# State-space stage: the power tables of three quarters, the norm-weight products and a mask product move from VectorE to GpSimd

## The chip, the cores and the metric

The kernel runs on one core of a Trainium2 chip. A core has a matrix engine (TensorE, PE in the profile), a vector engine (VectorE, DVE), a scalar engine (ScalarE, ACT), a general engine (GpSimd, POOL) and a queue engine that mostly issues transfers (SyncE, SP). Each engine takes its own instructions strictly in the order in which they stand in its program, and semaphores order the engines among each other. Data lies in SBUF (128 partitions), matmul results in PSUM. The metric is the device time of one execution in microseconds (us), smaller is better.

## The reference, cut to what matters

Two layers: a state-space (S5) mixer with a gated output projection, then a latent-attention mixer; each is followed by a gated MLP with a width-3 causal convolution. 256 tokens, 2048 channels, float32. The change touches only the first mixer:

```python
dt = exp(log_dt);  ab = exp(dt * a)                  # a complex, per group (128) and state (64)
bb = ((ab - 1) / a) * b                              # input matrix, 16 channels per group
h[t] = ab * h[t-1] + bb @ u[t]                       # u = rmsnorm(x) * g, per group of 16 channels
y[t] = Re(c @ h[t]) + d * u[t]
y = gelu(y);  val, gate = split(y @ w_glu + b_glu);  out = val * sigmoid(gate)
```

## The kernel before, in words

The recurrence is cut into blocks of 8 tokens. For such a block the kernel needs the powers of `ab` from 0 to 8 (times the coefficient of `bb`), called `z` and, copied with signs, `zs`. The 128 groups are handled in 16 rounds of 8 groups; four rounds make a quarter `qt`, and one call of `powers(qt)` makes the table `zs` for the four rounds of a quarter. `powers` is: two memsets on GpSimd, two ScalarE copies into `z`, then three doubling steps of four VectorE products, sums or differences each (12 instructions on 128 x 64 to 128 x 512 floats, each step reading what the last one wrote), and four ScalarE copies from `z` to `zs`.

A round `n` uses these helpers:

- `lead_e(n)` multiplies the table with the fetched matrices `bc[n]` on VectorE into `e1` and `e2` (128 x 1024 each), and a DMA issued by GpSimd adds `e2` onto `e1`. `lead_f(n)` makes `f1` and `f2` in the same way, and every second round the rotations `si`, `co`.
- `part_k(n)` builds the block kernel `K(n)` with TensorE from `f` and `bc`, ScalarE copies it out and writes it to DRAM (`kd`), and SP reads it back in another layout (`TP`).
- `part_e` and `part_v` transpose `e` (`ET`), multiply with the transposed input `U`, and ScalarE copies the result to `vs`. `part_r` and `part_h` rotate, scan and rotate back on VectorE (`R`, `H`). `part_c(n)` needs `TP(n)` and `H(n)`, two rounds after `part_k(n)`.
- After each quarter `part_d` applies the GELU, and matmuls of the output projection (`glu_steps`, weights 1 MB a unit, split by ScalarE into `whi` and by VectorE into `wlo`) fill TensorE between the rounds.

In the text below, K(1), vs(4) or e(9) are these tiles of round 1, 4 or 9; powers(1) is the table of the second quarter.

Ahead of the rounds ScalarE sums the squares of `x` (L135), GpSimd takes the power -1/2 of the mean (`pow` in `rstd`, L117), and `scale_x(rs, qt)` multiplies a quarter of `x` (two tiles X[0] and X[1], both tagged `raw`) by the norm's weights `gX` on VectorE (L358) and by `rs` on ScalarE (L362). The skip weights `dB` are multiplied with a mask (L341).

The order of the instructions on each engine is set when the program is built: a scheduler takes the operations as their inputs are due by its own costs, and `behind(ins)` forces an instruction to stand after another. At run time an engine that waits holds up everything that stands behind.

Of the kernel before, what the change touches and what calls it, by code (L numbers as in the profile page):

```python
# [12 lines left out]
ALU = mybir.AluOpType  # L13
AX = mybir.AxisListType

P = 128
# [28 lines left out]
def tile_trunk(ctx: ExitStack, tc: tile.TileContext, a: dict):  # L45
    nc = tc.nc
    act, dve, pool, pe, sync = nc.scalar, nc.vector, nc.gpsimd, nc.tensor, nc.sync
    cnt = [0]

    def T(pl, shape, dt=F32, tag=None, bufs=None):  # L50
        cnt[0] += 1
        kw = {"bufs": bufs} if bufs else {}
        return pl.tile(shape, dt, tag=tag, name=f"{tag}_{cnt[0]}", **kw)
# [3 lines left out]
    env = {"wp": ctx.enter_context(tc.tile_pool(name="wp", bufs=2)), "wb": 3}  # L57
# [12 lines left out]
    eps_half = cst[:, C_MH : C_MH + 8]  # L70

    def split(hi, lo, src, eng=None):
        act.activation(hi, src, AF.Copy)  # L73
        (eng or dve).tensor_tensor(lo, src, hi.bitcast(F32), op=ALU.subtract)  # L74

    def wunit(src, nk, cols, gain=None, heads=False, slots=(None, None), onpool=()):
        wp, nb = env["wp"], env["wb"]
        raw = T(wp, [P, nk, cols], F32, "raw")
        sync.dma_start(raw, src)
        out = []  # L80
        hk = max(nk // 2, 1)
        for i, h in enumerate(range(0, nk, hk)):
            if slots[i] is None:
                hi = T(wp, [P, hk, cols], F32R, "whi", nb)
                lo = T(wp, [P, hk, cols], F32R, "wlo", nb)
            else:
                pl = env["xp"] if slots[i] < 10 else env["yp"]
                both = T(pl, [P, 2, hk, cols], F32R, f"x{slots[i]}", 1)
                hi, lo = both[:, 0], both[:, 1]
            if heads:  # L90
                v = raw[:, h : h + hk, :].rearrange("p k (h e) -> p k h e", h=2)
                for o, w, e in ((0, 256, slice(0, P)), (256, 128, slice(P, 192))):
                    z = [t[:, :, o : o + w].rearrange("p k (h e) -> p k h e", h=2) for t in (hi, lo)]
                    split(*z, v[:, :, :, e])
            elif gain is None:
                split(hi, lo, raw[:, h : h + hk, :], pool if slots[i] in onpool else None)
            else:
                for k in range(hk):
                    g = gain[:, h + k : h + k + 1]
                    act.activation(hi[:, k, :], raw[:, h + k, :], AF.Copy, scale=g)  # L100
                    dve.scalar_tensor_tensor(
                        lo[:, k, :], raw[:, h + k, :], g, hi[:, k, :].bitcast(F32), op0=ALU.mult, op1=ALU.subtract
                    )
            out.append((hi, lo))
        return hk, out
# [7 lines left out]
    def rstd(tot, width, n):  # L113
        ms = T(sp, [P, width], F32, "rs_ms")
        dve.tensor_scalar(ms, tot, 1.0 / n, EPS, op0=ALU.mult, op1=ALU.add)
        y = T(sp, [P, width], F32, "rs_y")
        pool.tensor_tensor(y, ms, eps_half[:, :width], op=ALU.pow)  # L117
        t = T(sp, [P, width], F32, "rs_t")
        dve.tensor_tensor(t, y, y, op=ALU.mult)
        dve.tensor_tensor(t, t, ms, op=ALU.mult)  # L120
        dve.tensor_scalar(t, t, -0.5, 1.5, op0=ALU.mult, op1=ALU.add)
        r = T(sp, [P, width], F32, "rs_r")
        dve.tensor_tensor(r, t, y, op=ALU.mult)
        return r
# [55 lines left out]
    def behind(ins):  # L180
        return nullcontext() if ins is None else tc.issue_after(ins)
# [89 lines left out]
    def s5(f):  # L271
        with tc.tile_pool(name="s5", bufs=2) as q1, tc.tile_pool(name="dr", bufs=2, space=bass.MemoryType.DRAM) as dr:
# [6 lines left out]
            X = [T(w0, [P, 4, 512], F32, "raw") for _ in range(2)]  # L279
            for k in range(8):  # L280
                sync.dma_start(X[k // 4][:, k % 4, :], a["xs"][k])
            gX = T(q1, [P, 512], F32, "gX", 1)
# [6 lines left out]
            def t1(tag, w=1):  # L289
                return T(q1, [P, w, P], F32, tag, 1)  # L290
# [31 lines left out]
            for k in (1, 2, 4):  # L322
                u = t1("uu", 2)
# [14 lines left out]
            for z in Ds + Hs:  # L338
                pool.memset(z[:, :, 0:1], 0.0)
            dmask = cst[:, C_DM : C_DM + 16]  # L340
            dve.tensor_tensor(  # L341
                dB.rearrange("p (g q) -> p g q", q=16),
                dB.rearrange("p (g q) -> p g q", q=16),
                dmask.unsqueeze(1).to_broadcast([P, 32, 16]),
                op=ALU.mult,
# [9 lines left out]
            def scale_x(rs, qt):  # L355
                c = slice(P * qt, P * qt + P)
                for h in range(2):
                    dve.tensor_tensor(  # L358
                        X[h][:, :, c], X[h][:, :, c], gX[:, c].unsqueeze(1).to_broadcast([P, 4, P]), op=ALU.mult
                    )  # L360
                for s in range(8):
                    act.activation(  # L362
                        Xn[qt][:, :, 16 * s : 16 * s + 16],
                        X[s // 4][:, s % 4, c].rearrange("p (g q) -> p g q", q=16),
                        AF.Copy,
                        scale=rs[:, s : s + 1],
                    )

            def powers(qt):
                ps_ = slice(32 * qt, 32 * qt + 32)  # L370
                z = T(q1, [P, 2, 9, 2, 32], F32, "z", 1)
                pool.memset(z[:, 0, 8, 1, :], 1.0)
                pool.memset(z[:, 1, 8, 1, :], 0.0)
                act.activation(z[:, :, 8, 0, :], cf[:, :, ps_], AF.Copy)
                act.activation(z[:, :, 0, 1, :], L[8][:, :, ps_], AF.Copy)
                for k, o, i, m in ((1, 7, 8, 1), (2, 5, 7, 2), (4, 1, 5, 4)):

                    def v(b):
                        return z[:, :, b : b + m].rearrange("p c m t n -> p c (m t) n")

                    def l(c):
                        return L[k][:, c, ps_].unsqueeze(1).unsqueeze(1).to_broadcast([P, 2, 2 * m, 32])

                    u, w = (T(q1, [P, 2, 8, 32], F32, n, 1)[:, :, : 2 * m, :] for n in ("pu", "pw"))
                    dve.tensor_tensor(u, v(i), l(0), op=ALU.mult)
                    dve.tensor_tensor(w, v(i), l(1), op=ALU.mult)
                    dve.tensor_tensor(v(o)[:, 0], u[:, 0], w[:, 1], op=ALU.subtract)
                    dve.tensor_tensor(v(o)[:, 1], u[:, 1], w[:, 0], op=ALU.add)
                zz = T(q1, [P, 4, 8, 32], F32, "zs")
                act.activation(zz[:, 1], z[:, 1, 0:8, 1, :], AF.Copy, scale=cst[:, C_SG : C_SG + 1])  # L390
                act.activation(zz[:, 2], z[:, 0, 1:9, 0, :], AF.Copy, scale=cst[:, C_NSG : C_NSG + 1])
                act.activation(zz[:, 3], z[:, 1, 1:9, 0, :], AF.Copy, scale=-1.0)
                act.activation(zz[:, 0], z[:, 0, 0:8, 1, :], AF.Copy)
                return zz
# [16 lines left out]
            PB = 32 // NP  # L411
# [26 lines left out]
            def product(tag, bufs, sb, i):  # L438
                h = (sb % PB) * NP
                o = T(q1, [P, NP, 8, 16], F32, tag, bufs)  # L440
                zt = zs[sb // PB][:, i, :, h : h + NP].rearrange("p i n -> p n i").unsqueeze(3).to_broadcast([P, NP, 8, 16])
                dve.tensor_tensor(o, zt, bc[sb][:, i].unsqueeze(2).to_broadcast([P, NP, 8, 16]), op=ALU.mult)  # L442
                return o

            def fetch(n, eng):
                if n < nb:
                    bc[n] = T(q1, [P, 4, NP, 16], F32, "bc", 3)
                    eng.dma_start(bc[n], a["sBC"][n])

            def lead_e(n):  # L450
                if n >= nb:
                    return
                if n % PB == 0:
                    zs[n // PB] = powers(n // PB)
                E[n], e2 = product("e1", 3, n, 0), product("e2", 2, n, 1)
                pool.dma_start(E[n], e2, accum_op=ALU.add)

            def lead_f(n):
                if n >= nb:
                    return  # L460
                F[n] = product("f1", 3, n, 2), product("f2", 3, n, 3)
                if n % FR == 0:
                    si, co = frames(n // FR)
                    for k in range(FR):
                        fr[n + k] = (si[k], co[k])
# [117 lines left out]
            todo, zs, bc, E, F, fr, U, TP, ET, H = [], {}, {}, {}, {}, {}, {}, {}, {}, {}  # L583
            nb = 4 * PB
# [5 lines left out]
            rs = first_norm()  # L590
            for n in range(3):
                fetch(n, sync)
            lead_e(0)
            lead_f(0)
            scale_x(rs, 0)
# [496 lines left out]
    ng = a["norm_g"]  # L1092
    f = f_pair()
    todo = s5(f)
    env["ap"] = ctx.enter_context(tc.tile_pool(name="ap", bufs=1))
    env["xp"] = ctx.enter_context(tc.tile_pool(name="xp", bufs=1))
# [118 lines left out]
```

## Time and profile before

| what | value |
|---|---|
| median of 3 runs | 2155.88 us (2154.35 to 2156.42) |
| the profiled execution | 2150.99 us, span 2149.2 us |
| TensorE busy over the span | 2054.8 us (96%) |
| VectorE busy over the span | 1376.9 us (64%) |
| ScalarE busy over the span | 1093.6 us (51%) |
| GpSimd busy over the span | 32.3 us (2%), 73 instructions |
| granted TensorE clock, mean | 0.990 |

In timeline rows the columns are: start in us from the span's start, duration in us, engine, line, operation, tile written and tiles read, shape, count, and in brackets how long the engine was idle before and who ended that. Rows of groups have the busy sum and the mean in ns behind the bar. Rows of the table by stretch have, for each engine, its busy time and count in that stretch, then TensorE's granted clock and the transfers' share and rate. Lines are those of the kernel before; in the changed kernel the same operations stand two to three lines lower (L385 to L388 become L387 to L390, L485 becomes L487, L509 becomes L511).

### The profile page before, as it was taken

How to read it: one execution, taken by the hardware profiler on the slowest of the kernel's cores; microseconds unless marked ns; L12 is line 12 of the kernel's file. 1: busy time of each engine (PE TensorE's matmuls, PEld its weight loads, DVE VectorE, ACT ScalarE, POOL GpSimd, SP SyncE). 2: the span in 40 equal slices, each digit the busy share in tenths (PEclk: the TensorE clock that was granted, in tenths of full speed). 3: DMA queues.
4: the chain of work that ended last, by engine and by line, in shares of the span. 5: the costliest groups of instructions: out<-in, count | busy, mean ns of one | idle time of the engine just before them, and what ended most of it. 6: DMA issues, size and time to landing. Idle time of an engine off the chain costs nothing.

```text
span 2149.2 us, 30703 instructions
## 1 busy us (share of the span) xinstructions
PE 2054.8 (96%) x12372; PEld 1757.0 (82%) x12372; DVE 1376.9 (64%) x1931; ACT 1093.6 (51%) x1669; POOL 32.3 (2%) x73
## 2 busy tenths in 40 slices
PE   3789999999999999999999999999999999999998
PEld 2567777988888888888878998798888888888886
DVE  8998666665466556655685665666546655665567
ACT  6565445554455445534464555655545544553444
POOL 1000000000000000000000000000000000000000
PEclk9899999999999999999999999999999999999999
DMA  5777766455555565555564434545555655555654
GB/s 149 204 185 200 225 195 200 154 183 188 197 187 185 183 204 182 196 177 197 195 196 144 126 124 154 192 150 192 177 201 190 191 181 196 193 181 189 200 184 151
DMA packets 291966, 392.14 MB, mean 182 GB/s; under 512 B 10224, under 2 KB 205424, under 8 KB 291056
## 3 DMA queue, kind: packets, MB, share of 16 engines
q1 hardware_dynamic: 285344, 374.45, 53.4%
q0 software_dynamic: 2304, 8.39, 2.3%
q10 hardware_dynamic: 4176, 7.34, 0.9%
q8 instruction: 97, 1.59, 0.3%
q14 instruction: 45, 0.37, 0.1%
HBM read 375.73 MB, written 6.03 MB: 178 GB/s over the span
## 4 chain that ended last, share of the span: by engine, by line
PE 83%; DVE 7%; DMA 6%; ACT 2%; issue 1%; POOL 0%; ACTq 0%; SPq 0%; DVEq 0%; POOLq 0%
PE wk L737 29%; PE wk L739 15%; PE acc L110 10%; PE acc L108 10%; PE acc L109 10%; DMA raw<-in_w_glu 2%; PE wk L109 2%; PE wk L110 2%; PE wk L108 2%; DVE wlo L74 1%; DMA bc<-in_sBC 1%; PE wk L419 1%; ACT whi L73 1%; DVE e L442 1%; DVE f L442 1%
## 5 line engine op out<-in xcount | busy, mean ns | idle before, releaser
L74 DVE TENSOR_TENSOR wlo<-raw,whi 128x1024 fp32r<-128x1024 f32 (+1 forms) x636 | 756.1, 1191 | 603.0 <-ACT whi L73 599.4
L73 ACT ACTIVATE whi<-raw 128x1024 fp32r<-128x1024 f32 (+1 forms) x636 | 654.2, 1032 | 756.0 <-PE wk L737 324.4
L737 PE MATMUL wk<-act,whi 128*128 128x512 f32 x2688 | 673.5, 392 | 0.0
L737 PEld LDWEIGHTS wk<-act,whi 128*128 128x128 f32 x2688 | 483.9, 189 | 86.7
L739 PEld LDWEIGHTS wk<-act,wlo 128*128 128x128 f32 x2688 | 366.7, 190 | 26.2
L739 PE MATMUL wk<-act,wlo 128*128 128x256 f32 x2688 | 374.8, 282 | 0.0
L109 PE MATMUL acc<-wlo,hh 128*128 128x512 f32 x652 | 255.9, 392 | 0.0
L110 PE MATMUL acc<-whi,hl 128*128 128x512 f32 x652 | 255.2, 393 | 0.0
L108 PE MATMUL acc<-whi,hh 128*128 128x512 f32 x652 | 253.7, 389 | 0.0
L109 PEld LDWEIGHTS acc<-wlo,hh 128*128 128x128 f32 x652 | 122.4, 188 | 27.6 <-DVE wlo L74 0.2
L108 PEld LDWEIGHTS acc<-whi,hh 128*128 128x128 f32 x652 | 122.4, 188 | 27.7 <-ACT hh L73 0.5
L110 PEld LDWEIGHTS acc<-whi,hl 128*128 128x128 f32 x652 | 122.5, 188 | 25.0
L108 PE MATMUL acc<-whi,act 128*128 128x512 f32 (+1 forms) x316 | 121.8, 387 | 1.9 <-ACT act L73 1.7
L110 PE MATMUL acc<-whi,act 128*128 128x512 f32 (+1 forms) x316 | 119.2, 378 | 0.6 <-DVE act L74 0.6
L109 PE MATMUL acc<-wlo,act 128*128 128x512 f32 (+1 forms) x316 | 119.1, 378 | 0.2 <-DVE wlo L74 0.2
L796 DVE SCALAR_TENSOR_TENSOR cv<-gs,cw,cv 128x255 f32<-128x255 f32 (+1 forms) x168 | 81.0, 482 | 17.2 <-ACT cv L794 14.3
L794 ACT ACTIVATE cv<-gs,cb,cw 128x256 f32<-128x256 f32 x84 | 49.9, 594 | 46.1 <-DVE gs L745 46.1
L108 PEld LDWEIGHTS acc<-whi,act 128*128 128x128 f32 x316 | 60.0, 190 | 13.9 <-ACT act L73 3.1
L110 PEld LDWEIGHTS acc<-whi,act 128*128 128x128 f32 x316 | 59.9, 190 | 12.4 <-DVE act L74 1.5
L109 PEld LDWEIGHTS acc<-wlo,act 128*128 128x128 f32 x316 | 60.0, 190 | 11.3 <-DVE wlo L74 1.1
L74 DVE TENSOR_TENSOR x<-raw,x 128x1024 fp32r<-128x1024 f32 x36 | 43.2, 1220 | 31.0 <-ACT x L73 31.0
L108 PE MATMUL acc<-x,act 128*128 128x512 f32 (+1 forms) x164 | 57.4, 352 | 5.6 <-DVE act L197 3.6
(278 smaller groups left out, 2247.3 us busy)
## 6 DMA issues: line engine op xcount, KB each, us to landing
raw<-in_w_gate SPq DMA_DIRECT2D x88, 1024.0 KB
raw<-in_w_up SPq DMA_DIRECT2D x88, 1024.0 KB
raw<-in_w_down SPq DMA_DIRECT2D x88, 1024.0 KB
raw<-in_w_glu SPq DMA_DIRECT2D x32, 1024.0 KB
raw<-in_w_o SPq DMA_DIRECT2D x16, 1024.0 KB
e<-e POOLq DMA_DIRECT2D x16, 512.0 KB, 6.0
TP<-kd SPq DMA_DIRECT2D x64, 128.0 KB
raw<-in_w_ukv SPq DMA_DIRECT2D x8, 1024.0 KB
```

The source lines that it names most:

```text
L73: act.activation(hi, src, AF.Copy)
L74: (eng or dve).tensor_tensor(lo, src, hi.bitcast(F32), op=ALU.subtract)
L108: pe.matmul(o, lh, rh, start=first, stop=False)
L109: pe.matmul(o, lh, rl, start=False, stop=False)
L110: pe.matmul(o, ll, rh, start=False, stop=last)
L419: pe.matmul(o[32 * j : 32 * j + 32, g * P : (g + 1) * P], lhs(g, j), rhs(g, j), start=g == 0 and i == 0, stop=diag is None and g == NG - 1 ...
L442: dve.tensor_tensor(o, zt, bc[sb][:, i].unsqueeze(2).to_broadcast([P, NP, 8, 16]), op=ALU.mult)
L737: pe.matmul(o, w, pair(kt), start=kt == 0, stop=False)
L739: pe.matmul(o[:, 0, :], w, pair(kt)[:, 0], start=False, stop=kt == KT - 1)
L794: act.activation(cv[:, ft, :], gv[:, ft, :], AF.Identity, scale=cw[:, 2, n : n + 1], bias=cb[:, n : n + 1])
L796: dve.scalar_tensor_tensor(cv[:, ft, sh:], gv[:, ft, : S - sh], cw[:, 2 - sh, n : n + 1], cv[:, ft, sh:], op0=ALU.mult, op1=ALU.add,)
```

## The change

All eight products of `x` with `gX`, the mask product of `dB`, and the twelve instructions of `powers` for quarters 2, 3 and 4 are issued on GpSimd. Quarter 1 stays on VectorE. powers(q) for q = 1, 2, 3 is now called in `lead_e` of rounds 1, 5 and 9 and is put behind the DMA of that round's `e`; the products of X[1] are put behind `pow`. An argument of `wunit` that no caller used is dropped (not shown).

```diff
@@ rstd
-        pool.tensor_tensor(y, ms, eps_half[:, :width], op=ALU.pow)
+        env["root"] = pool.tensor_tensor(y, ms, eps_half[:, :width], op=ALU.pow).ins
@@ s5
-            dve.tensor_tensor(
+            pool.tensor_tensor(
                 dB.rearrange("p (g q) -> p g q", q=16),
...
             def scale_x(rs, qt):
                 c = slice(P * qt, P * qt + P)
                 for h in range(2):
-                    dve.tensor_tensor(
-                        X[h][:, :, c], X[h][:, :, c], gX[:, c].unsqueeze(1).to_broadcast([P, 4, P]), op=ALU.mult
-                    )
+                    with behind(env["root"] if h else None):
+                        pool.tensor_tensor(
+                            X[h][:, :, c], X[h][:, :, c], gX[:, c].unsqueeze(1).to_broadcast([P, 4, P]), op=ALU.mult
+                        )
...
-            def powers(qt):
+            def powers(qt, eng, after=None):
...
-                pool.memset(z[:, 0, 8, 1, :], 1.0)
+                with behind(after):
+                    pool.memset(z[:, 0, 8, 1, :], 1.0)
...
-                    dve.tensor_tensor(u, v(i), l(0), op=ALU.mult)
-                    dve.tensor_tensor(w, v(i), l(1), op=ALU.mult)
-                    dve.tensor_tensor(v(o)[:, 0], u[:, 0], w[:, 1], op=ALU.subtract)
-                    dve.tensor_tensor(v(o)[:, 1], u[:, 1], w[:, 0], op=ALU.add)
+                    eng.tensor_tensor(u, v(i), l(0), op=ALU.mult)
+                    eng.tensor_tensor(w, v(i), l(1), op=ALU.mult)
+                    eng.tensor_tensor(v(o)[:, 0], u[:, 0], w[:, 1], op=ALU.subtract)
+                    eng.tensor_tensor(v(o)[:, 1], u[:, 1], w[:, 0], op=ALU.add)
...
             def lead_e(n):
                 if n >= nb:
                     return
-                if n % PB == 0:
-                    zs[n // PB] = powers(n // PB)
                 E[n], e2 = product("e1", 3, n, 0), product("e2", 2, n, 1)
-                pool.dma_start(E[n], e2, accum_op=ALU.add)
+                ins = pool.dma_start(E[n], e2, accum_op=ALU.add).ins
+                if n % PB == 1 and n + 3 < nb:
+                    zs[n // PB + 1] = powers(n // PB + 1, pool, ins)
...
             for n in range(3):
                 fetch(n, sync)
+            zs[0] = powers(0, dve)
             lead_e(0)
```

The scheduler moves other instructions with it. GpSimd's own row, from its first product to the DMA of round 2, before (`e_71`, `e_86`, `e_90` are e(0), e(1), e(2)):

```order
L117 TENSOR_TENSOR rs_y_205<-rs_ms_203,cst_73 128x8
L372 MEMSET z_577 128x32
L373 MEMSET z_577 128x32
L456 DMA e_71_247<-e_72_249 128x1024
L456 DMA e_86_323<-e_87_325 128x1024
L456 DMA e_90_332<-e_91_334 128x1024
```

The same stretch now, up to the third of the twelve instructions of powers(1) (`raw_96` is X[0], `raw_97` is X[1], `z_328` is the table of powers(1)):

```order
L359 TENSOR_TENSOR raw_96<-raw_96,gX_106 128x4x128 x2
L341 TENSOR_TENSOR dB_107<-dB_107,cst_73 128x512
L359 TENSOR_TENSOR raw_96<-raw_96,gX_106 128x4x128 x2
L117 TENSOR_TENSOR rs_y_205<-rs_ms_203,cst_73 128x8
L359 TENSOR_TENSOR raw_97<-raw_97,gX_106 128x4x128 x4
L375 MEMSET z_328 128x32
L456 DMA e_71_247<-e_72_249 128x1024
L456 DMA e_86_323<-e_87_325 128x1024
L374 MEMSET z_328 128x32
L387 TENSOR_TENSOR pu_333<-z_328,L_32_146 128x2x64
L388 TENSOR_TENSOR pw_334<-z_328,L_32_146 128x2x64
L389 TENSOR_TENSOR z_328<-pu_333,pw_334 128x64
```

The other nine follow, and only then the DMA of round 2. Five products now stand ahead of `pow`, four behind it, and all of powers(1) stands between the DMAs of rounds 1 and 2. In the same way powers(2) stands between the DMAs of rounds 5 and 6, and powers(3) between those of rounds 9 and 10.

ScalarE in round 1, before (`K_46` is K(1), `kd_399` its way to DRAM, `U_375` is U(1)); here the copies `zs` of powers(1) stand in round 3:

```order
L473 ACTIVATE U_375<-wk_372 128x256
L448 DMA bc_406<-in_sBC 128x512
L485 ACTIVATE K_46_185<-wk_377 128x2x128
L503 ACTIVATE ET_408<-wk_409 128x512
L487 DMA kd_399<-K_46_185 128x480
```

ScalarE in round 1 now (`zs_351` is the table of powers(1), `U_403` is U(1), `kd_427` the way of K(1) to DRAM):

```order
L475 ACTIVATE U_403<-wk_400 128x256
L363 ACTIVATE act_54_200<-raw_97,rs_r_211 128x8x16 x2
L393 ACTIVATE zs_351<-z_328,cst_73 128x256
L392 ACTIVATE zs_351<-z_328,cst_73 128x256
L394 ACTIVATE zs_351<-z_328 128x256
L395 ACTIVATE zs_351<-z_328 128x256
L487 ACTIVATE K_46_185<-wk_405 128x2x128
L450 DMA bc_434<-in_sBC 128x512
L489 DMA kd_427<-K_46_185 128x480
L505 ACTIVATE ET_436<-wk_437 128x512
```

The four copies of powers(1) have moved two rounds forward and stand right ahead of K(1) and of its DMA.

ScalarE in round 5 now (`ET_849` is ET(4), `zs_757` the table of powers(2), `vs_887` is vs(4)); before, `vs(4)` followed `ET(4)` and the copy `dc` directly:

```order
L505 ACTIVATE ET_849<-wk_850 128x512
L489 DMA kd_840<-K_45_184 128x480
L505 ACTIVATE ET_849<-wk_856 128x512
L527 ACTIVATE dc_48_189<-mag_20_118 128x8x31
L393 ACTIVATE zs_757<-z_734,cst_73 128x256
L392 ACTIVATE zs_757<-z_734,cst_73 128x256
L394 ACTIVATE zs_757<-z_734 128x256
L395 ACTIVATE zs_757<-z_734 128x256
L511 ACTIVATE vs_887<-wk_878 128x2x128
```

The copies of powers(2) now stand between ET(4) and vs(4); those of powers(3) stand between ET(7) and vs(7) in the same way.

More of the change, by code (lines that the diff above doesn't have):

```diff
@@ L74, in split, with wunit @@
         (eng or dve).tensor_tensor(lo, src, hi.bitcast(F32), op=ALU.subtract)
-    def wunit(src, nk, cols, gain=None, heads=False, slots=(None, None), onpool=()):
+    def wunit(src, nk, cols, gain=None, heads=False, slots=(None, None)):
         wp, nb = env["wp"], env["wb"]
@@ L95, in wunit @@
             elif gain is None:
-                split(hi, lo, raw[:, h : h + hk, :], pool if slots[i] in onpool else None)
+                split(hi, lo, raw[:, h : h + hk, :])
             else:
```

## The prediction

> **What bounds the kernel now.** I read the table by stretch first, because the change touches only the first tenth of the span. Its rows give, for each stretch, the busy time of PE, PEld, DVE, ACT and POOL, then the granted clock and the transfers.
>
> ```profile
> 0.00:240.00 240.00, 175.68 (x2238) 137.78 (x2239) 205.55 (x347) 139.71 (x289) 18.08 (x41) 0.96 0.67 183
> 400.00:2149.20 1749.20, 1727.56 (x9379) 1494.15 (x9377) 1068.26 (x1426) 870.45 (x1248) 10.97 (x25) 1.00 0.55 181
> ...
> 26.90:58.60 31.70, 18.81 (x263) 13.82 (x263) 28.97 (x46) 13.69 (x40) 3.84 (x6) 0.94 0.73 177
> 62.00:120.00 58.00, 46.47 (x611) 36.60 (x610) 55.97 (x87) 37.03 (x77) 5.58 (x10) 0.91 0.72 188
> 120.00:155.00 35.00, 26.93 (x348) 20.21 (x350) 30.02 (x50) 23.50 (x43) 1.74 (x2) 1.00 0.69 186
> 155.00:240.00 85.00, 78.77 (x979) 63.39 (x971) 70.02 (x106) 45.36 (x79) 3.61 (x6) 0.97 0.67 185
> ```
>
> After 400 us TensorE is busy 1727.56 of 1749.2 us, so nothing there gives back what the first 240 us lose or win. In the state-space stage VectorE sets the pace: 28.97 of 31.7 us, then 55.97 of 58; from 155 us on TensorE is the fuller one (78.77 of 85). An instruction taken off VectorE can count before 120 us, by half up to 155, and little after that.
>
> **What leaves VectorE.** These groups lie in the first 240 us; busy sum and mean ns stand behind the bar.
>
> ```profile
> L385 DVE TENSOR_TENSOR pu<-z,L 128x128 f32<-128x128 f32 (+2 forms) x12 | 5.5, 462 | 0.1
> L386 DVE TENSOR_TENSOR pw<-z,L 128x128 f32<-128x128 f32 (+2 forms) x12 | 5.5, 462 | 0.0
> L387 DVE TENSOR_TENSOR z<-pu,pw 128x64 f32<-128x64 f32 (+2 forms) x12 | 3.7, 307 | 0.1
> L388 DVE TENSOR_TENSOR z<-pu,pw 128x64 f32<-128x64 f32 (+2 forms) x12 | 3.7, 306 | 0.0
> L358 DVE TENSOR_TENSOR raw<-raw,gX 128x512 f32<-128x512 f32 x8 | 5.4, 683 | 0.0
> L341 DVE TENSOR_TENSOR dB<-dB,cst 128x512 f32<-128x512 f32 x1 | 0.7, 685 | 0.0
> ...
> 48.01 1.29 DVE L358 TENSOR_TENSOR raw<-raw,gX 128x512 f32<-128x512 f32 x2
> ```
>
> Four quarters of powers cost 5.5 + 5.5 + 3.7 + 3.7 = 18.4 us, so 4.6 us a quarter; three go, 13.8 us, with 5.4 and 0.7 us of products: 19.9 us in all. Neighbours overlap by 0.08 us (two products take 1.29, not 1.37 us), so a quarter occupies 3.7 us of VectorE's time, a product 0.6.
>
> Where that lies on the path:
>
> - Start: six L358 and L341, 4.2 us, stand ahead of the first `f`. I count 0 (from -2.5 gained to +0.4 lost), worked out below.
> - powers(1): 3.7 us stand around a wait of 3.23 us for TensorE (next rows), so VectorE only waits more. But e(4) had to wait for this table, and the scan R (L529) behind it. In the new order VectorE has only one `e` product, one `f` product and three small instructions between the wait's end and R: 2 x 1.14 + 3 x 0.34 = 3.3 us (rows of 1.22 and 0.42 less the overlap) instead of 7.1 (62.09 to 69.22). TensorE sat 5.4 us for R. Gain 3.5, a little under the 3.8 difference since the deferred work comes back.
> - powers(2) runs from 94.31 to 99.84 us, where VectorE is full: gain 3.7.
> - powers(3) begins at 136.66 us, in the stretch that counts by half: gain 1.9.
> - Two L358 at 48 us stand in the same shadow of the wait as powers(1): 0.
>
> ```profile
> 58.59 0.42 PE L419 MATMUL wk<-TP,U 128*32 128x128 f32 x1 [1.21 <-DMA TP<-kd]
> 62.09 0.42 DVE L521 TENSOR_TENSOR w<-wk,co 128x256 f32<-128x256 f32 x1 [3.23 <-PE wk L519]
> 65.47 2.36 DVE L442 TENSOR_TENSOR e<-zs,bc 128x1024 f32<-128x1024 f32 x2 [0.83 <-ACT zs L390]
> 69.22 0.69 DVE L529 TENSOR_TENSOR_SCAN R<-dc,w 128x256 f32<-128x256 f32 x1
> 70.06 1.19 PE L534 MATMUL wk<-R,cst 128*128 128x256 f32 x2 [5.42 <-DVE R L529]
> ...
> 94.31 0.27 DVE L385 TENSOR_TENSOR pu<-z,L 128x128 f32<-128x128 f32 x1
> 99.42 0.42 DVE L388 TENSOR_TENSOR z<-pu,pw 128x256 f32<-128x256 f32 x1
> 136.66 0.28 DVE L385 TENSOR_TENSOR pu<-z,L 128x128 f32<-128x128 f32 x1
> ```
>
> Sum of gains 9.1 us.
>
> **What it costs on GpSimd.** The trace has no GpSimd product of this size. From below I bound a quarter by VectorE's 4.6 us; nothing shown makes GpSimd faster. From above:
>
> ```profile
> L632 POOL MEMSET krE<- 128x256 f32 x1 | 0.3, 312 | 0.3 <-POOLq L1205 0.3
> L339 POOL MEMSET dc<- 128x8 f32 x2 | 0.2, 113 | 0.0
> 371.27 1.22 DVE L74 TENSOR_TENSOR x<-raw,x 128x1024 fp32r<-128x1024 f32 x1
> 371.43 1.46 POOL L143 TENSOR_TENSOR rs_y<-tot,cst 128x1 f32<-128x1 f32 x1 [9.49 <-DVE tot L141]
> 2132.38 0.54 POOL L143 TENSOR_TENSOR rs_y<-tot,cst 128x1 f32<-128x1 f32 x1 [723.51 <-DVE tot L141]
> 2132.44 0.69 DVE L163 TENSOR_TENSOR f<-f,gb 128x512 f32<-128x512 f32 x1
> ```
>
> One written stream costs (312 - 113) / 248 = 0.80 ns an element. Two inputs and an output taken one after another make 2.4 ns. A quarter has 2688 elements a partition in twelve instructions: 6.5 us, and 12 times a fixed part between 0.11 (the small memset) and 0.54 us (the one-element power): 7.8 to 12.9 us. I take 7.8, a plain product being nearer to a memset than to a power, and 1.35 us for a 512-wide product.
>
> Then there is the waiting. The power that met a VectorE instruction with two SBUF inputs (371.27 + 1.22 = 372.49) ended 0.40 us behind it, after 1.46 us instead of 0.54; the one at 2132.38, issued just ahead of one, took 0.54. So GpSimd waits until such an instruction is done. VectorE's mean instruction is 28.97 / 46 = 0.63 us in the stretch of powers(1); half to all of one before each of the twelve is 3.8 to 7.6 us. I take 5.7, which makes powers(1) 13.5 us, and 10 us for the later two, where VectorE runs dry part of the time (it waits for what ScalarE holds back).
>
> The Trainium skill (SBUF — State Buffer, "SBUF: two separate sides") says that GpSimd and a VectorE instruction with two SBUF inputs take a shared port pair as an exclusive lock for the whole instruction. The row at 371.43 agrees for GpSimd as the loser; no run here shows VectorE as the loser. By it the rival "both stall" below would hold.
>
> The skill (GPSIMD Engine Reference, "Performance versus the Vector engine") has GpSimd's `tensor_tensor` at 1.96 times VectorE's time; an estimate from that page for a quarter is 9.0 us, and with it alone and no waiting the change would about break even by the formula below.
>
> **Who waits for it.** GpSimd works in order, and so does ScalarE, whose copies `zs` now stand ahead of K(1), vs(4) and vs(7).
>
> ```profile
> 34.06 0.86 POOL L456 DMA_DIRECT2D e<-e  x1 [2.33 <-DVE e L442]
> 38.58 0.86 POOL L456 DMA_DIRECT2D e<-e  x1 [3.66 <-DVE e L442]
> 43.38 0.41 ACT L485 ACTIVATE K<-wk 128x256 f32<-128x256 f32 x1 [1.90 <-DVE w L523]
> 64.92 0.52 ACT L390 ACTIVATE zs<-z,cst 128x256 f32<-128x256 f32 x1
> 66.03 0.42 ACT L393 ACTIVATE zs<-z 128x256 f32<-128x256 f32 x1
> ...
> 74.89 0.86 POOL L456 DMA_DIRECT2D e<-e  x1 [5.59 <-DVE e L442]
> 80.61 0.38 ACT L509 ACTIVATE vs<-wk 128x256 f32<-128x256 f32 x1 [1.24 <-PE wk L419]
> ...
> 113.97 0.86 POOL L456 DMA_DIRECT2D e<-e  x1 [5.36 <-PE wk L426]
> 123.09 0.38 ACT L509 ACTIVATE vs<-wk 128x256 f32<-128x256 f32 x1
> ```
>
> The copies last 66.03 + 0.42 - 64.92 = 1.5 us.
>
> - powers(1): GpSimd is free after e(1) at 34.06 + 0.86 = 34.9; + 13.5 + 1.5 = 49.9 for K(1), against 43.38: 6.5 us late. Behind K(1) is its way through DRAM, and TensorE already waited for that (58.59 us row), then VectorE for TensorE (62.09). All of it is on the path. The DMA of e(2), issued at 38.58 before, comes at 48.4, inside nearly the same delay.
> - powers(2): e(5) at 74.89 + 0.86 + 10 + 1.5 = 87.3 for vs(4), against 80.61: 6.7 us, with no idle time on VectorE to cover it.
> - powers(3): e(9) at 113.97 + 0.86 + 10 + 1.5 = 126.3 for vs(7), against 123.09: 3.2 us.
>
> Sum 16.4. With 9.1 gained, the forecast is +7.3 us. With one time q for every quarter, the costs are (q - 7.0) + (q - 3.4) + (q - 6.8), so the change breaks even at 3q = 26.3, q = 8.8 us.
>
> The start:
>
> ```profile
> 11.91 0.19 ACT L135 ACTIVATION_READ_ACCUMULATOR junk<-raw 128x1 f32 x1
> 17.51 1.76 POOL L117 TENSOR_TENSOR rs_y<-rs_ms,cst 128x8 f32<-128x8 f32 x1 [15.44 <-DVE rs_ms L115]
> 20.74 3.32 ACT L362 ACTIVATE act<-raw,rs_r 128x128 f32<-128x128 f32 x11 [1.67 <-DVE rs_r L123]
> 26.03 0.51 ACT L391 ACTIVATE zs<-z,cst 128x256 f32<-128x256 f32 x1
> ```
>
> X[0] is free for the products at 12.1 us, after its last sum of squares. Five products at 1.35 plus 0.3 of waiting end at 20.4, so the power starts 2.9 us later than at 17.51. ScalarE has nine of the scalings by `rs` ahead of the first table's copies: 20.74 + 2.9 + 9 x 0.30 = 26.4 against 26.03. VectorE's 4.2 us are free, but ScalarE isn't ready: -2.5 without the late power, +0.4 with it. I take 0.
>
> **The sum.** The profiled execution took 2150.99 us (span 2149.2), 4.9 us under the median of the runs, 2155.88; the run-to-run spread is 2 us. I add the 7.3 us to the median: 2163 us. Changes within 0.2%, 4.3 us, are what a measurement of this kernel cannot tell from none.
>
> **Rivals.**
>
> 1. GpSimd as fast as VectorE and unhindered (q = 4.6): only vs(4) is late, by 1.2 us; the start gains 2.5. Sum -9.1 - 2.5 + 1.2 = -10.4, 2145.5 us. For it: GpSimd is busy 18 of the first 240 us, and VectorE is full. Against it: the row at 371.43. It turns into a gain from q under 8.8, a measurable one under 7.3.
> 2. GpSimd at its own pace of 7.8 us but seldom hindered: 0.8 + 4.4 + 1.0 - 9.1 = -2.9, 2153 us, no change to be told. For it: VectorE also reads PSUM and pauses, and the powers could slip into these places.
> 3. Both stall: VectorE also waits while GpSimd reads. Nine products at 1.35 us, four fifths of them against two-input work, cost VectorE 9.7 us in the start, of which 4.2 were freed: +5.5; powers(1) 6.2 less the 3.2 idle: +3.0; powers(2) +2.5 in the 4 us before VectorE runs dry. With 7.3 that is +18, 2174 us. For it: the waiting shown is of such a kind; against it: VectorE's 0.69 us at 2132.44 is no longer than its 0.683.
>
> **Chances.** Forecast (q of 10 to 13.5) 0.39; rival 1 0.30; rival 2 0.21; rival 3 0.10. Of the forecast 0.06 falls within 0.2%, of rival 2 a quarter is faster. So faster 0.35, same 0.22, slower 0.43. The range to hold the time eight times in ten runs from 2147, in the middle of rival 1, to 2174, rival 3; the forecast's own is 2158 to 2169.
>
> **What would show it.** In the changed profile: the twelve GpSimd instructions of powers(1) from the DMA of e(1) to the first copy `zs` (13.5 us; under 8.8 and I am wrong); the wait of ScalarE's `zs` copies for GpSimd (about 6 us ahead of K(1), 7 ahead of vs(4), 3 ahead of vs(7)); K(1) near 50 us; two-input VectorE rows at their 1.22 us (longer, up to 2.4, is rival 3); the power at 20.4 us. The forecast fails if ScalarE does not wait at those three places, or if the rounds after 155 us, where TensorE is fuller, take back the delay.

## The result, and the profile after

The changed kernel takes 2185.13 us, median of 4 runs (2182.98 to 2187.89), against 2156.15 us of the kernel before on the same chip: a ratio of 1.014, 95% interval 1.0124 to 1.0156, or +30 us (27 to 34). The direction was forecast, the size was not: 2163 us was predicted, 2174 the upper end. The profiled execution took 2184.58 us, with a span of 2182.8 us, 33.6 us over the span of before.

The table by stretch of the changed kernel, to be read against the rows of the prediction:

```profile
0.00:240.00 240.00, 150.73 (x1846) 116.22 (x1849) 181.05 (x265) 123.99 (x264) 69.41 (x86) 0.89 0.60 160
400.00:2182.80 1782.80, 1756.85 (x9622) 1521.62 (x9621) 1089.38 (x1478) 889.30 (x1295) 13.15 (x29) 1.00 0.55 180
155.00:240.00 85.00, 74.10 (x857) 58.27 (x858) 69.00 (x102) 48.86 (x86) 4.49 (x7) 0.93 0.64 176
```

In the first 240 us TensorE is busy 150.73 us instead of 175.68. The 25 us that are missing come later: behind 400 us it is busy 29 us more than before (1756.85 against 1727.56) and as full as it was (of 1782.8 us). VectorE is busy 181.05 us instead of 205.55, and GpSimd 69.41 instead of 18.08. The work did move, and the stage as a whole became slower. The clock granted to TensorE in these 240 us is 0.89 instead of 0.96; no run here separates what that adds to the loss.

GpSimd in the changed kernel: the start, then the first, some middle and the last of the twelve instructions of powers(1), powers(2) and powers(3).

```profile
12.69 3.02 POOL L359 TENSOR_TENSOR raw<-raw,gX 128x512 f32<-128x512 f32 x2 [10.62 <-DMA gkv<-in_gkv]
23.05 1.84 POOL L117 TENSOR_TENSOR rs_y<-rs_ms,cst 128x8 f32<-128x8 f32 x1 [3.31 <-DVE rs_ms L115]
41.73 3.46 POOL L387 TENSOR_TENSOR pu<-z,L 128x128 f32<-128x128 f32 x1
45.16 0.44 POOL L388 TENSOR_TENSOR pw<-z,L 128x128 f32<-128x128 f32 x1
45.68 0.32 POOL L389 TENSOR_TENSOR z<-pu,pw 128x64 f32<-128x64 f32 x1
46.35 0.72 POOL L387 TENSOR_TENSOR pu<-z,L 128x256 f32<-128x256 f32 x1
47.84 0.46 POOL L389 TENSOR_TENSOR z<-pu,pw 128x128 f32<-128x128 f32 x1
54.34 1.70 POOL L390 TENSOR_TENSOR z<-pu,pw 128x256 f32<-128x256 f32 x1
...
86.95 2.46 POOL L387 TENSOR_TENSOR pu<-z,L 128x128 f32<-128x128 f32 x1
95.08 1.26 POOL L387 TENSOR_TENSOR pu<-z,L 128x512 f32<-128x512 f32 x1
97.64 0.72 POOL L389 TENSOR_TENSOR z<-pu,pw 128x256 f32<-128x256 f32 x1
98.32 0.72 POOL L390 TENSOR_TENSOR z<-pu,pw 128x256 f32<-128x256 f32 x1
...
135.72 3.00 POOL L387 TENSOR_TENSOR pu<-z,L 128x128 f32<-128x128 f32 x1
148.64 0.72 POOL L390 TENSOR_TENSOR z<-pu,pw 128x256 f32<-128x256 f32 x1
```

The short rows of each size are GpSimd's own pace: 2 x (0.44 + 0.32 + 0.72 + 0.46 + 1.26 + 0.72) = 7.8 us for a quarter, the value that the prediction took. With the waiting a quarter took 14.3 us (41.73 to 56.04), 12.1 (86.95 to 99.04) and 13.6 (135.72 to 149.36), where the prediction had 13.5, 10 and 10.

VectorE in the changed kernel, at the start and beside powers(1):

```profile
14.52 1.28 DVE L315 TENSOR_SCALAR w<-L 128x128 f32<-128x128 f32 x1
18.54 1.48 DVE L324 TENSOR_TENSOR uu<-L 128x256 f32<-128x256 f32 x1
23.09 0.28 DVE L388 TENSOR_TENSOR pw<-z,L 128x128 f32<-128x128 f32 x1
24.92 1.22 DVE L119 TENSOR_TENSOR rs_t<-rs_y 128x8 f32<-128x8 f32 x1 [1.55 <-POOL rs_y L117]
33.43 1.23 DVE L444 TENSOR_TENSOR f<-zs,bc 128x1024 f32<-128x1024 f32 x1 [0.28 <-ACT zs L393]
42.52 2.35 DVE L444 TENSOR_TENSOR e<-zs,bc 128x1024 f32<-128x1024 f32 x2
47.45 0.42 DVE L523 TENSOR_TENSOR w<-wk,co 128x256 f32<-128x256 f32 x1 [2.57 <-PE wk L521]
49.90 2.29 DVE L444 TENSOR_TENSOR f<-zs,bc 128x1024 f32<-128x1024 f32 x1
52.12 1.74 DVE L531 TENSOR_TENSOR_SCAN R<-dc,w 128x256 f32<-128x256 f32 x1
```

Four of them in the kernel before:

```profile
13.36 0.22 DVE L315 TENSOR_SCALAR w<-L 128x128 f32<-128x128 f32 x1
14.17 0.42 DVE L324 TENSOR_TENSOR uu<-L 128x256 f32<-128x256 f32 x1
19.30 0.17 DVE L119 TENSOR_TENSOR rs_t<-rs_y 128x8 f32<-128x8 f32 x1 [1.14 <-POOL rs_y L117]
26.86 1.22 DVE L442 TENSOR_TENSOR f<-zs,bc 128x1024 f32<-128x1024 f32 x1
```

These rows answer the question that the prediction left to its third rival: VectorE waits for GpSimd too. Beside GpSimd's products `f` takes 2.29 us instead of 1.22, the scan 1.74 instead of 0.69, the 128x8 product `rs_t` 1.22 instead of 0.17, the `TENSOR_SCALAR` 1.28 instead of 0.22 and `uu` 1.48 instead of 0.42. `w<-wk,co`, which has an input in PSUM, keeps its 0.42 us.

ScalarE in the changed kernel, at the three places that the prediction named:

```profile
54.41 0.51 ACT L393 ACTIVATE zs<-z,cst 128x256 f32<-128x256 f32 x1 [5.79 <-POOL z L389]
57.10 0.38 ACT L487 ACTIVATE K<-wk 128x256 f32<-128x256 f32 x1
...
98.40 0.51 ACT L393 ACTIVATE zs<-z,cst 128x256 f32<-128x256 f32 x1 [8.28 <-POOL z L389]
100.11 0.36 ACT L511 ACTIVATE vs<-wk 128x256 f32<-128x256 f32 x1
...
149.39 0.51 ACT L392 ACTIVATE zs<-z,cst 128x256 f32<-128x256 f32 x1 [10.85 <-POOL z L390]
152.52 1.04 ACT L73 ACTIVATE whi<-raw 128x1024 fp32r<-128x1024 f32 x1
153.94 0.37 ACT L511 ACTIVATE vs<-wk 128x256 f32<-128x256 f32 x1
```

All three waits are there. Against before, the delay grows as follows: 6.6 us at the first `f` (33.43 against 26.86), 13.7 at K(1) (57.10 against 43.38), 19.5 at vs(4) (100.11 against 80.61), 30.9 at vs(7) (153.94 against 123.09), and 33.6 at the end of the spans.

### The profile page after: what moved, and what is told of

It reads as the page before. It is cut to its first block, busy times and chain, and to the rows that moved or that the text cites. A ratio compares the mean times of both kernels' runs of the same rounds, so it can differ in the third digit from the quotient of the medians.

```text
span 2182.8 us, 30700 instructions
## 1 busy us (share of the span) xinstructions
PE 2058.0 (94%) x12372; PEld 1757.1 (80%) x12372; DVE 1376.1 (63%) x1886; ACT 1093.4 (50%) x1669; POOL 83.7 (4%) x118
## 4 chain that ended last, share of the span: by engine, by line
PE 79%; DMA 5%; DVE 5%; ACT 3%; issue 1%; POOL 0%; DVEq 0%; POOLq 0%; ACTq 0%; SPq 0%
PE wk L740 28%; PE wk L742 14%; PE acc L110 9%; PE acc L109 9%; PE acc L108 9%; DMA raw<-in_w_glu 2%; PE wk L109 2%; PE wk L108 2%; PE wk L110 2%; DMA bc<-in_sBC 1%; DVE wlo L74 1%; ACT whi L73 1%; PE wk L421 1%; DVE x L74 1%; DMA raw<-in_w_dkv 1%
## 5 line engine op out<-in xcount | busy, mean ns | idle before, releaser
L799 DVE SCALAR_TENSOR_TENSOR cv<-gs,cw,cv 128x255 f32<-128x255 f32 (+1 forms) x168 | 81.0, 482 | 17.2 <-ACT cv L797 14.3
L143 POOL TENSOR_TENSOR rs_y<-tot,cst 128x1 f32<-128x1 f32 x18 | 13.7, 760 | 1931.9 <-DVE tot L141 1209.2
```

What stands on the lines that cost most here:

```text
L143: pool.tensor_tensor(y, t, eps_half[:, 0:1], op=ALU.pow)
L799: dve.scalar_tensor_tensor(cv[:, ft, sh:], gv[:, ft, : S - sh], cw[:, 2 - sh, n : n + 1], cv[:, ft, sh:], op0=ALU.mult, op1=ALU.add,)
```

## The experiments

Theory 1: the loss is ScalarE standing in order behind `zs` copies that wait for GpSimd, plus a late start. Theory 2: the loss is VectorE and GpSimd blocking each other, and the DMAs of e(2), e(6), e(10) that stand behind the powers on GpSimd, wherever the copies stand. All ratios are against the kernel before on the same chip; us are the ratio's excess times 2156.

| kernel | ratio | 95% interval | us |
|---|---|---|---|
| changed kernel | 1.0140 | 1.0124 to 1.0156 | +30.2 |
| e1 products alone | 1.0033 | 1.0023 to 1.0044 | +7.1 |
| e2 powers alone | 1.0090 | 1.0077 to 1.0104 | +19.4 |
| e3 changed, `zs` written down later | 1.0084 | 1.0071 to 1.0098 | +18.1 |
| e4 before, twelve scratch products on GpSimd | 1.0028 | 1.0017 to 1.0040 | +6.0 |
| e5 e2, `zs` tied | 1.0020 | 1.0010 to 1.0031 | +4.3 |
| e6 before, memsets on GpSimd | 1.0010 | 0.9996 to 1.0023 | +2.2 |
| e7 e1, all products behind the power | 1.0049 | 1.0031 to 1.0066 | +10.6 |
| e8 e2 without quarter 4 | 1.0009 | 0.9999 to 1.0020 | +1.9 |
| e9 changed, `zs` of quarter 4 tied | 1.0064 | 1.0049 to 1.0079 | +13.8 |
| e10 e5, powers spread | 1.0030 | 1.0018 to 1.0042 | +6.5 |
| e11 e8, `zs` tied | 1.0007 | 0.9996 to 1.0018 | +1.5 |
| e12 quarter 2 alone, all `zs` tied | 0.9971 | 0.9960 to 0.9982 | -6.3 |
| e13 nothing moved, all `zs` tied | 0.9981 | 0.9969 to 0.9993 | -4.1 |
| e14 quarter 2 alone, its `zs` tied | 0.9965 | 0.9951 to 0.9979 | -7.5 |

**e1, products alone.** The changed kernel with `powers` back on VectorE at its old place:

```diff
-                if n % PB == 1 and n + 3 < nb:
-                    zs[n // PB + 1] = powers(n // PB + 1, pool, ins)
+                if n % PB == 0 and n:            # ahead of the e products
+                    zs[n // PB] = powers(n // PB, dve)
```

> The nine products (eight of x with the norm's weights, one of dB with its mask) on GpSimd, all four tables of powers on VectorE as before. The start of the changed kernel is 6.6 us later at the first f product. If that start is one of the causes: the first f again near 33 us and the time 4 to 7 us over the kernel before (about 2161). If the rounds behind it take the delay back, or if the start term of the prediction (0) holds at the end: within 2 us of the kernel before.

+7.1 us, and the first `f` as late as in the changed kernel:

```profile
33.25 1.23 DVE L444 TENSOR_TENSOR f<-zs,bc 128x1024 f32<-128x1024 f32 x1 [0.28 <-ACT zs L393]
```

The start is a cause of its own, and the rounds behind it do not take it back.

**e2, powers alone.** The products and the mask return to VectorE:

```diff
-                        pool.tensor_tensor(X[h][:, :, c], ...
+                        dve.tensor_tensor(X[h][:, :, c], ...
-            pool.tensor_tensor(dB...
+            dve.tensor_tensor(dB...
```

> Powers of quarters 2 to 4 on GpSimd, the nine products on VectorE as before. If start and powers add up, and e1 shows 4 to 7 us: +22 to +25 us over the kernel before (about 2180), with ScalarE waiting for the powers ahead of K(1), vs(4) and vs(7). If the later start was what made the powers late: +10 us or less.

+19.4 us, a little under the range expected. With e1's 7.1 that makes 26.5, just under the changed kernel's 27 to 34. ScalarE waits for the powers ahead of K(1) and, for 10.90 us, ahead of vs(7). Ahead of vs(4), where the expectation had a wait too, the copies follow without one:

```profile
87.93 0.49 ACT L393 ACTIVATE zs<-z,cst 128x256 f32<-128x256 f32 x1
```

So of the three waits of the changed kernel, the one at vs(4) is there only together with the moved products.

**e3, the copies written down later.** `powers` ends before its four `zs` copies, and these are called in `lead_e(4q)`:

```diff
+            def table(z):
                 zz = T(q1, [P, 4, 8, 32], F32, "zs")
...
+                if n % PB == 0 and n:
+                    zs[n // PB] = table(zs[n // PB])
                 E[n], e2 = product("e1", 3, n, 0), product("e2", 2, n, 1)
```

> The changed kernel with the four zs copies of a quarter written down three rounds later, ahead of the first e product that reads them; GpSimd's work is the same. Theory 1 (ScalarE, in order behind these copies, carries the delay at K(1), vs(4), vs(7)): the three waits of 7, 8 and 11 us go, about 22 us come back, some 2163 us, of which the start is what is left. Theory 2 (the delay is VectorE stalled beside GpSimd, and the DMAs of e(2), e(6), e(10) that stand behind the powers in GpSimd's queue): less than 8 us come back, 2177 us or more.

12 us came back, between what the two theories expected. The experiment did not do what its edit says: the scheduler put copies ahead of vs(1) and of vs(7) (the next expectation calls it vs(5)), and there two of them still waited, as its table of waits says (total us, times, longest):

```profile
ACT zs L395 <- POOL z L390: 8.0, 2, 4.1
```

It decides nothing by itself; e5 does it over.

**e4 and e6, GpSimd working for nobody.** The kernel before, with instructions on GpSimd whose results nobody reads, behind the DMAs of e(1), e(5), e(9): in e4 twelve products of a quarter's sizes, in e6 memsets:

```diff
+                for w in (128, 128, 64, 64, 256, 256, 128, 128, 512, 512, 256, 256):     # e4
+                    pool.tensor_tensor(u[:, :w], gX[:, :w], gX[:, :w], op=ALU.mult)
+                for w in 24 * (512,):                                                    # e6
+                    pool.memset(u[:, :w], 0.0)
```

> The kernel before, and beside it GpSimd makes twelve products of the sizes of a quarter's powers, into scratch, behind the DMAs of e(1), e(5) and e(9); nobody waits for the results, and VectorE's work is all there. Left out: nothing. Theory 1: no ScalarE wait, so only the DMAs of e(2), e(6), e(10) and a few longer VectorE rows: +8 us or less. Theory 2: most of the 22 to 25 us is there without any wait for a table: +15 us or more. VectorE rows with SBUF operands should be stretched from 1.22 to about 2 us beside them.

> The kernel before, and GpSimd writes zeros into scratch, 24 memsets of 512 elements (about 12.5 us), at the places of e4's twelve products. It holds the DMAs of e(2), e(6), e(10) as long as e4 does, but reads nothing. If reading two SBUF inputs is what stops VectorE: VectorE rows with SBUF operands stay at 1.22 us and the time within 2 us of the kernel before. If the held DMAs are what e4's 6 us are: again +4 to +8 us.

e4 costs 6.0 us though nothing is taken from VectorE and nothing waits for a result; e6 cannot be told from no change. VectorE's rows show what differs. First e4, `f` and the scan beside products:

```profile
43.35 2.06 DVE L449 TENSOR_TENSOR f<-zs,bc 128x1024 f32<-128x1024 f32 x1
45.33 1.52 DVE L538 TENSOR_TENSOR_SCAN R<-dc,w 128x256 f32<-128x256 f32 x1
```

Then e6, memsets from 39.14 us on, and `f` beside them:

```profile
39.14 6.10 POOL L400 MEMSET su<- 128x512 f32 x10
42.48 1.22 DVE L449 TENSOR_TENSOR f<-zs,bc 128x1024 f32<-128x1024 f32 x1
```

Beside products `f` takes 2.06 us, beside memsets, which read nothing, 1.22. The Trainium skill (SBUF — State Buffer, "SBUF: two separate sides") says this: an exclusive lock for the whole instruction, against a VectorE instruction with two SBUF inputs only where GpSimd's instruction reads SBUF; both rows agree. What e6 doesn't show is the part of the held DMAs: the scheduler let the DMA of e(2) slip in between the memsets at 38.60 us, against 47.20 in e4, and those of e(6) and e(10) likewise. So e4's 6.0 us are not parted into stalls of VectorE and held DMAs.

**e5, the copies tied.** e2 with the table split as in e3, and each `zs` copy put behind the second `ET` copy of the round ahead of its use:

```diff
+                    env["et"] = act.activation(ET[:, 4 * w : 4 * w + 4, :], ptv, AF.Copy).ins
...
+                with behind(env.get("et")):
                     act.activation(zz[:, 1], ...
```

> Powers of quarters 2 to 4 on GpSimd, products on VectorE, and the zs copies of a quarter tied behind the second ET copy of the round ahead of their first use (in e3 two of the three places still waited 4.1 us each, since they had only slid to just ahead of vs(1) and vs(5)). Theory 1 (ScalarE's in-order wait is the whole cost of the powers): no zs copy waits, the 19.8 us of e2 fall to the stalls of e4 (+6.6) less the gains of the prediction (-9.1): 2150 to 2158 us. Theory 2 (stalls and held DMAs of e(2), e(6), e(10) matter as much): 2164 us or more.

+4.3 us: 15.1 of e2's 19.4 us are gone while GpSimd does the same work. ScalarE's table of waits for 20 to 160 us has no `zs` that waits for GpSimd any more. The time is just above the range of theory 1 and far below theory 2. VectorE in e5:

```profile
64.31 0.69 DVE L540 TENSOR_TENSOR_SCAN R<-dc,w 128x256 f32<-128x256 f32 x1
75.14 2.32 DVE L451 TENSOR_TENSOR f<-zs,bc 128x1024 f32<-128x1024 f32 x1 [5.73 <-PE wk L428]
```

This R is R(2), the third scan (the expectation of e11 calls it R(3)). It comes 4.9 us before its 69.22 of the kernel before: at this place the gain of 3.5 forecast for powers(1) is real. A wait for TensorE of 5.73 us follows from 69.4 us on, and at vs(4) e5 is 4.1 us late (84.73 against 80.61).

**e7, all products behind the power.** e1 with `behind(env["root"])` on all nine products.

> e1 with all nine products on GpSimd behind the power of the first norm instead of five ahead of it. If the late power (23.05 against 17.51 us) is what makes the start late: the power at 17.5, first f within 3 us of before's 26.9, time 2156 to 2160 us. If VectorE's stalls beside the products do it: still +6 us (2163), now with the e products and f products stretched.

+10.6 us: the late power is not the cause. In the rows (GpSimd first, then VectorE) the power starts at 17.58, as before, and `f` is as late as in e1:

```profile
17.58 1.83 POOL L117 TENSOR_TENSOR rs_y<-rs_ms,cst 128x8 f32<-128x8 f32 x1 [15.51 <-DVE rs_ms L115]
...
19.44 1.23 DVE L119 TENSOR_TENSOR rs_t<-rs_y 128x8 f32<-128x8 f32 x1 [1.54 <-POOL rs_y L117]
32.89 1.23 DVE L447 TENSOR_TENSOR f<-zs,bc 128x1024 f32<-128x1024 f32 x1 [0.24 <-ACT zs L396]
```

The first `zs` copy on ScalarE, which `f` needs, waits 4.82 us for the table that VectorE makes beside GpSimd's products:

```profile
32.35 0.51 ACT L396 ACTIVATE zs<-z,cst 128x256 f32<-128x256 f32 x1 [4.82 <-DVE z L392]
```

In both places that were tried for the nine products, VectorE's chain to the first `f` stops for them.

**e8, without quarter 4.** e2 with `n + 7 < nb`, so that the last table is made by VectorE as before.

> e2 with powers of quarters 2 and 3 on GpSimd and those of quarter 4 on VectorE as before. If vs(7) is the dearest of the three places (+12.5 us in the changed kernel, against 3.2 in the prediction): 9 to 13 us under e2, about 2165. If the rounds behind 155 us, where TensorE is fuller, would have taken that delay back: at most 4 us under e2.

+1.9 us: quarter 4 alone is worth 19.4 - 1.9 = 17.5 us, more than expected. vs(7) of e2 and of e8:

```profile
143.85 0.37 ACT L511 ACTIVATE vs<-wk 128x256 f32<-128x256 f32 x1
```

```profile
132.10 0.38 ACT L513 ACTIVATE vs<-wk 128x256 f32<-128x256 f32 x1
```

That is 11.8 us of the 17.5. The second thing that e8 shows is what becomes of the earlier delay, of which the wait ahead of K(1) is the start (as in e2, no copy waits ahead of vs(4)). It is 9.0 us behind the kernel before at vs(7) (132.10 against 123.09), but only 4.9 us when SP issues the last round's `TP`, first before, then e8:

```profile
224.48 2.47 SPq L491 DMA_DIRECT2D TP<-kd  x4
```

```profile
229.37 2.47 SPq L495 DMA_DIRECT2D TP<-kd  x4
```

The table by stretch has where it was made good, e8 first, then e2:

```profile
155.00:240.00 85.00, 82.75 (x1026) 66.79 (x1024) 76.30 (x118) 49.67 (x89) 3.58 (x6) 1.00 0.67 185
```

```profile
155.00:240.00 85.00, 72.39 (x880) 57.55 (x880) 69.17 (x104) 47.85 (x84) 4.49 (x7) 0.96 0.65 173
```

Before, TensorE was busy 78.77 of these 85 us; e8 fills 82.75, at a granted clock of 1.00 instead of 0.97, and catches up. e2 fills 72.39. Its table of waits has, for 160 to 250 us, a row that e8's doesn't have:

```profile
PE wk L421 <- DVE H L545: 7.1, 3, 2.6
```

TensorE waits 7.1 us for `H` there. In the kernel before this wait was 2.3 us. The scheduler, with no powers of quarter 4 to place on VectorE, has ordered VectorE's products and `H` otherwise in these rounds. That this order is the remaining 6 us is likely, but was not tried by itself.

**e9, only quarter 4 tied.** The changed kernel whole, with the tie of e5 on quarter 4's copies alone:

```diff
-                    zs[n // PB + 1] = powers(n // PB + 1, pool, ins)
+                    zs[n // PB + 1] = powers(n // PB + 1, pool, ins)
+                    if n // PB < 2:
+                        zs[n // PB + 1] = table(zs[n // PB + 1])
...
+                if n == 3 * PB:
+                    zs[n // PB] = table(zs[n // PB], env["et"])
```

> The changed kernel whole, products and all three quarters of powers on GpSimd, with only quarter 4's zs copies tied behind the second ET copy of round 10. e8 gave back 17.5 of e2's 19.8 us by leaving quarter 4 on VectorE. If the wait of its first zs copy (10.85 us, with si, co, two f copies and a whi queued behind it on ScalarE) is that cost: 13 to 17 us under the changed kernel, about 2170. If it is GpSimd's work of quarter 4 itself (VectorE held beside it, 13.6 us): at most 5 us, about 2180.

+13.8 us, 16.4 less than the changed kernel, with GpSimd still making all three quarters. vs(7) comes at 142.83 us instead of 153.94:

```profile
142.83 0.38 ACT L522 ACTIVATE vs<-wk 128x256 f32<-128x256 f32 x1
```

The place of four copies in ScalarE's queue is about half of the change's loss of 30.2.

**e10, spread.** e5 with `powers` cut into its three steps, one behind each of the DMAs of e(4q-3), e(4q-2), e(4q-1).

> e5 with the three steps of a quarter's powers cut apart, one behind each of the DMAs of e(4q-3), e(4q-2), e(4q-1), so that no DMA waits for more than four products. Left in e5 are +4 us; if these are the held DMAs of e(2), e(6), e(10): 2150 to 2155 us, no slower than the kernel before. If they are VectorE's stalls, which the spreading does not lessen: 2157 to 2160.

+6.5 us, above both ranges and no better than e5, though the DMA of e(2) is issued at 40.44 us instead of 49.46. So the held DMA of e(2) is not what e5 has left. That VectorE's stalls beside the powers are, as the other branch of the expectation has it, remains likely and not shown.

**e11, e12, e13, e14: what is left of the gain.** From e5, with `n + 7 < nb` (e11: quarters 2 and 3 on GpSimd), `n + 11 < nb` (e12: quarter 2), no powers on GpSimd at all (e13), and e12 with the tie on quarter 2 alone (e14):

```diff
+                if n == 1:                                                   # e14
+                    zs[1] = powers(1, pool, ins)
...
+                if n % PB == 0 and n:
+                    zs[n // PB] = table(zs[1], env["et"]) if n == PB else table(powers(n // PB, dve))
```

> Quarters 2 and 3 on GpSimd as in e8, with their zs copies (and those of quarter 4, whose powers stay on VectorE) tied as in e5. If the tie is worth at K(1) and vs(4) what it is at vs(7): R(3) 5 us earlier than in the kernel before instead of 2 us earlier, and 2148 to 2154 us. If TensorE takes back early gains as it took back e8's early delays (9 us at vs(7), 2 at the end): 2154 to 2158.

> Only quarter 2's powers on GpSimd, where VectorE waits 3.2 us for TensorE and e(4) waits for the table; all zs copies tied as in e5. The prediction's gain at this place was 3.5 us; if it is real and kept: 2150 to 2153 us. If the work behind takes it back: within 2 us of the kernel before.

> All powers and products on VectorE as in the kernel before, and the zs copies of quarters 2 to 4 tied behind the second ET copy of rounds 2, 6 and 10, as in e12. If e12's gain of 5.7 us is GpSimd's: within 2 us of the kernel before. If it is the tie's: 2149 to 2152 us.

> Quarter 2's powers on GpSimd, its zs copies tied, those of quarters 3 and 4 untied and their powers on VectorE as before. If the gain is that of moving quarter 2: 2149 to 2153 us as e12. If the ties of quarters 3 and 4 bring it: 2154 to 2158.

e11 shows no gain. No copy waits for GpSimd in it, while e8 has the wait ahead of K(1), and the two end alike (+1.5 and +1.9): that wait costs nothing at the end that can be told. e12 and e14 are faster than both kernels; e14 takes 2148.03 us, 0.35% less than before (0.21 to 0.49). e13 says that the tie of quarters 3 and 4 is worth something by itself, 4.1 us (1.5 to 6.7), which was not expected if the gain were GpSimd's alone; the medians alone differ by 2.2 us, and the one traced run of e13 is 2.0 us late at its last `TP` (226.51 against 224.48), so where these us arise is open. But e14 has neither of these ties and still has 7.5 (4.5 to 10.6). For quarter 2 with its powers on VectorE the tie changes no order (its copies stood between the two ET copies of round 3 already), so e14's gain comes of quarter 2 on GpSimd, with the order that the scheduler then makes; the two are not parted. In e14 R(2) is 4.8 us early:

```profile
64.41 0.69 DVE L540 TENSOR_TENSOR_SCAN R<-dc,w 128x256 f32<-128x256 f32 x1
...
76.78 0.42 DVE L532 TENSOR_TENSOR w<-wk,co 128x256 f32<-128x256 f32 x1 [6.56 <-PE wk L530]
```

Soon after, a wait of 6.56 us eats it, and vs(4) is 1.5 us late (82.13 against 80.61). At the last `TP` the kernel is 2.9 us early (221.55 against 224.48). So how the early gain becomes 7.5 us at the end was measured but not followed.

## Why the prediction was wrong

By the prediction's own groups, its terms against what the runs showed for the same group:

| group | predicted | measured |
|---|---|---|
| the start (nine products) | 0 | +7.1 (e1) |
| powers(1) and powers(2): -3.5 + 6.5 - 3.7 + 6.7 | +6.0 | +1.9 (e8) |
| powers(3): -1.9 + 3.2 | +1.3 | +17.5 (e2 less e8) |

- **The step on ScalarE's order was right for the changed kernel.** ScalarE waits at K(1), vs(4) and vs(7) for GpSimd. The delay grew by 7.1 us from the first `f` to K(1) (6.5 forecast) and by 8.7 from the copy `dc` right ahead to vs(4) (6.7). e5 shows that the place of the copies, not the work on GpSimd, is 15.1 of the 19.4 us that the powers lose; e8, e9 and e11 put it on the wait ahead of vs(7).
- **The start failed.** "VectorE's 4.2 us are free, but ScalarE isn't ready" counted GpSimd's waiting and not VectorE's. Four instructions from L315 to L324 end at 20.02 us instead of 14.59, so the power came at 23.05, not 20.4; behind it the four small steps of `rstd` took 1.22 us each instead of 0.17. The third rival had +5.5 us for the start by this mechanism; the trace has 6.6. Its chance of 0.10 was too low. The row held against it, 0.69 us at 2132.44, was no test of products: it stands beside a power, and in the changed kernel, too, a product of VectorE beside the power (`pw` at 23.09, beside 23.05) keeps its 0.28 us. The sentence of the Trainium skill cited there (SBUF — State Buffer, "SBUF: two separate sides"), by which rival 3 would hold, was borne out.
- **powers(3) failed, and is the largest error.** Its 10 us were 13.6, and the 1.5 us of copies behind them were 4.55 (149.39 to 153.94), because `si`, `co`, two copies of `f` and a `whi` had collected behind the waiting copy. The gain of 1.9 us is not seen. So 3.2 us late became 10.6 in the changed kernel (20.2 us behind at ET(7), 30.9 at vs(7)) and 11.8 between e8 and e2, and the rounds behind made it 17.5.
- **Adding each delay through to the end failed** for powers(1) and powers(2): 9 us at vs(7) in e8 are 1.9 at the end, because TensorE had room behind 155 us. In e8 no copy waits ahead of vs(4), and the delay grows only from 7.1 us at K(1) to 9.0 at vs(7). The prediction named the rounds behind 155 us only as a way to be wrong. The two errors, one too dear and one too cheap, did not cancel.
- **The price of GpSimd was right** (7.8 us unhindered, 12 to 14 with waiting), and with it rivals 1 and 2 fell. **The gain of powers(1)** was right in kind: R(2) is 4.9 us early in e5, once ScalarE doesn't wait.

## What to carry to other kernels

When work is moved to a slower engine ahead of its use, look first at who consumes it in order: a copy that is issued as soon as its input is written down blocks everything behind it on its own engine, and tying it to its place of use gave back 15 of 19 us here without touching the work. Then move little, where there is slack: one quarter of four, tied, was a gain of 0.35%; three were a loss of 0.2% tied and of 0.9% untied. A delay is worth what the next full engine makes of it, so price each at the end and not at the place where it arises.

## What the hardware showed

- The blocking between VectorE and GpSimd goes both ways and hits small instructions hardest: a 128x8 product went from 0.17 to 1.22 us, one GpSimd product of 512. A `TENSOR_SCALAR` with one SBUF input is hit as well (0.22 to 1.28 us), an instruction with a PSUM input is not (0.42).
- GpSimd doesn't always get its turn after one instruction: the first 128x128 product of powers(1), issued at 41.73 us, ended at 45.19, right behind the last of VectorE's back-to-back products (42.52 + 2.35 = 44.87), 3.46 us for 0.44 us of work.
- Memsets on GpSimd (0.6 us for 512 elements) left VectorE's two-input products at 1.22 us.
